# Tail of a hybrid layer issued by two parts of the tokens, and its low-rank products as two split passes on 128 rows

## The chip, the core and the metric

The kernel runs on one core of one Trainium2 chip. The metric is the device time of the whole program in microseconds (us). TensorE (PE) multiplies, with PEld as its weight loads; VectorE (DVE), ScalarE (ACT) and GpSimd (POOL) do the elementwise work; SyncE (SP) mostly issues DMA transfers.

## The reference

Two layers over 768 tokens (256 of context, then 512 latents); the second layer needs its output for the latents alone. D = 1024, D_FF = 4096.

```python
for l in range(DEPTH):                       # DEPTH = 2
    h = modulate(x, norm_mix_pre[l], shift0, scale0)          # rms_norm(x, g) * (1 + scale) + shift
    o = token_mixer(h, ...)     # w_in -> rwkv (decay, iclr: low-rank), conv, attention -> w_branch, gates, w_out
    x = x + mod2 * rms_norm(o, norm_mix_post[l])
    h = modulate(x, norm_mlp_pre[l], shift1, scale1)
    x = x + mod5 * rms_norm(square(relu(h @ w_ff1[l])) @ w_ff2[l], norm_mlp_post[l])
# low-rank, d = 0, 1:  w_raw = w0[d] + tanh(wd) @ w2[d];  a = sigmoid(a0[d] + ad @ a2[d])   (64 x 1024 each)
```

Context and latents have modulation vectors of their own. The output is the latents' x in float32.

## The kernel before

Activations lie transposed, channels on the partitions in KT = 8 tiles of 128, tokens along the free axis. A layer has T = 768 tokens (layer 0) or 512 (layer 1, the latents alone).

**Large products.** Every large product is done as three fp32r products of parts that are each rounded: weight-hi by activation-hi (`wh`, `hh`), weight-hi by activation-lo (`hl`), weight-lo (`wl`) by activation-hi. One job is one output tile of 128 channels: 8 k-tiles, 3 products each, over one or two pieces of the tokens (2 x 384 in layer 0, one of 512 in layer 1). `gemm` (L378, product L389) issues a whole job; `job` and `fill` (L392 to L414, product L412) keep jobs in a list, from which other parts of the program take a few k-steps at a time, so that products lie between other work.

**Weights.** A job takes two weight halves (`weight_half`, L369): an SP DMA of 256 KB into `raw` (L372), a ring of two buffers; ACT rounds it into `wh` (L328); DVE subtracts to get `wl` (L332). `wh` and `wl` have three buffers each. A slot of `raw` is free again after the DVE subtraction.

**The tail of a layer.** `merge_phase` (L1237) ends with the 8 jobs of `w_out` into `acc`. Then, in `mlp_phase` (L1335): load X (the residual stream) from DRAM, post-norm with gate and add to X, sums of squares of X, norm and modulation into `hh`, `hl` (`norm_h`, L334, its first step L343), 4 quarters q of the MLP (8 jobs of `w_ff1`, 8 of `w_ff2` each), post-norm and add again, and in layer 0 the norm for layer 1 and the store of X to DRAM (`xT_d`, L1392), in layer 1 the transposes and the store of the output (`store_x`). Row sums of squares go through PE by a vector of ones (L311; squares by ACT at L306 and L320). `rstd` (L281) takes them to ACT (L287), PE (L291), DVE (L279) and back by PE transposes (L298) as `mm`; the post-norm is a DVE scalar_tensor_tensor (L359) and an add (L361) on DVE or POOL. In `mlp_phase` all of this is for all tokens at once. The mod steps (L234: a `wmod` load of 1 MB and 4 products each) make the next layer's modulation, one after each job of `w_ff1`.

**The low-rank products.** For each of 8 head pairs and each layer `rw_open` (L1021) loads `lw` (two DMAs on SP, L1025), and `rw_lora` (L1028, product L1032) multiplies 64 rows of `lw` (one direction) by 64 rows of `low`, in float32.

**Spills.** 36 output tiles of `w_in` (queries, keys, values, gates) are made as jobs between the steps of the rwkv branch and written to a DRAM tensor `z` (`spill`, L1155).

The order is that of the Python program, on which a tile framework's scheduler then settles each engine's order.

Of the kernel before, what the change touches and what calls it, by code (L numbers as in the profile page):

```python
# [76 lines left out]
class Kern:  # L77
# [255 lines left out]

    def norm_h(s, sp, X, R, T, gs, sh, hh, hl):  # L334

        nc = s.nc
        o = TOK - T
        for k in range(KT):
            t = sp.tile([128, TOK], F32, tag="nt", name="nt", bufs=2)
            for b, t0, t1 in s.pieces(T, CTX):  # L340
                v = 1 if t0 < CTX else 0
                sl = slice(t0, t1)
                nc.vector.scalar_tensor_tensor(out=t[:, sl], in0=X[:, k, sl], scalar=gs[:, k, v:v + 1], in1=R[:, b, :t1 - t0], op0=ALU.mult, op1=ALU.mult)  # L343
                if k % 2:
                    nc.scalar.activation(out=t[:, sl], in_=t[:, sl], func=AF.Identity, bias=sh[:, k, v:v + 1])
                else:
                    nc.scalar.activation(out=hh[:, k, sl], in_=t[:, sl], func=AF.Identity, bias=sh[:, k, v:v + 1])  # L347
                    nc.vector.scalar_tensor_tensor(out=hl[:, k, sl], in0=t[:, sl], scalar=sh[:, k, v:v + 1], in1=hh[:, k, sl].bitcast(F32), op0=ALU.add, op1=ALU.subtract)
            if k % 2:
                s.split(hh[:, k, o:], hl[:, k, o:], t[:, o:], True)  # L350

    def post_norm(s, sp, A, X, R, T, gm, each):

        nc = s.nc
        o = TOK - T
        for k in range(KT):
# [35 lines left out]
    def job(s, src, mh, ml, T, done, pre=None):  # L392

        s.halves += [(src, h) for h in range(2)]
        s.jobs += [(k, mh, ml, T, done, pre) for k in range(KT)]

    def fill(s, n=1):
        nc = s.nc
        for _ in range(min(n, len(s.jobs))):
            k, mh, ml, T, done, pre = s.jobs.pop(0)  # L400
# [243 lines left out]
    def stage(s):  # L644
        return s.wp.tile([128, TOK], F32, tag="f0", name="f0", bufs=2)
# [25 lines left out]
    def rw_loras(s, l, P, T):  # L671
        nc = s.nc
        s.sgd = s.rp.tile([128, TOK], F32, name="sgd")
        s.low = s.rp.tile([128, 2, TOK], F32, name="low")
        s.shift_mix(l, P, C_WD, TOK, lambda: s.low[:, 0])
        s.shift_mix(l, P, C_AD, TOK, lambda: s.low[:, 1])
        s.shift_mix(l, P, C_GD, T, lambda: s.sgd)
        s.fill(24)
        nc.scalar.activation(out=s.low[:, 0], in_=s.low[:, 0], func=AF.Tanh)
# [341 lines left out]
    def rw_open(s, l, p):  # L1021

        lw = s.rt("lw", [128, 2, 128])
        for i, n in ((0, 'rw_w2'), (1, 'rw_a2')):
            s.nc.sync.dma_start(lw[:, i, :], s.i[n][l, :, :, 128 * p:128 * p + 128].rearrange("d r n -> (d r) n"))  # L1025
# [37 lines left out]
    def spill(s, l, r, T):  # L1063

        c0, t, f = s.spills[r]
        T = TOK if t else T
        s.in_job(l, c0, T, lambda ps: s.spill_done(r, T, f, ps))

    def spill_done(s, r, T, tanh, ps):
        nc = s.nc  # L1070
        ft = s.stage()
        if tanh:
            nc.scalar.activation(out=s.dv(ft, T), in_=s.pv(ps, T), func=AF.Tanh, scale=0.5)
        else:
            nc.scalar.activation(out=s.dv(ft, T), in_=s.pv(ps, T), func=AF.Copy)
        nc.scalar.dma_start(s.z[128 * r:128 * r + 128, TOK - T:], ft[:, TOK - T:])


    def run(s):
# [13 lines left out]
        s.z = s.dp.tile([128 * len(s.spills), TOK], F32, name="z")  # L1093
        s.kp = lambda d: d.rearrange("(k p) t -> p k t", p=128)
# [15 lines left out]
        for l in range(DEPTH):  # L1110
# [5 lines left out]
            s.h_open()  # L1116
            s.mlp_phase(l, PP, T, acc, actx)
# [9 lines left out]
    def rwkv_phase(s, l, P, T):  # L1127
# [3 lines left out]
        with ExitStack() as rc:  # L1131
# [105 lines left out]
    def merge_phase(s, l, PP, T, acc):  # L1237
# [4 lines left out]
        with ExitStack() as mc:  # L1242
# [67 lines left out]
            drive(ln, 3)  # L1310
            s.fill(len(s.jobs))
            branch(1, *operand(lambda k: cvx[k]))
            for j in range(KT):
                s.fill(8)
                if steps:
                    steps.pop(0)()
            for k in range(KT):
                nc.vector.tensor_scalar(out=acc[:, k, o:], in0=acc[:, k, o:], scalar1=0.5, scalar2=None, op0=ALU.mult)
            hs, ls = operand(lambda k: acc[:, k])
            s.ss = s.ps2()  # L1320

            def done(j, ps):
                nc.scalar.activation(out=s.dv(acc[:, j], T), in_=s.pv(ps, T), func=AF.Copy)
                s.ss_slow(lp, s.ss, acc[:, j], j, T)
            for j in range(KT):
# [121 lines left out]
```

## Time and profile before

| | |
|---|---|
| median of 3 runs | 4390.17 us (4380.69 to 4404.21) |
| the profiled execution | 4402.83 us, span 4401.0 us |
| PE busy | 4180.3 us, 95% of the span |
| DVE, ACT, POOL busy | 2707.6, 1819.4, 289.9 us |

The profile holds one execution. A span is what lies between its first and its last instruction; the time of the execution is 1.8 us longer. Busy time is summed by engine, and "the chain" is the work that ended last, followed back step by step.

### The profile page before, as it was taken

The page shows a single profiled execution, that of the slowest core. Times are in us where ns is not written, and L with a number is a line of the kernel's source. Part 1 is how long each engine was busy: PE and PEld are TensorE (multiplying, and loading weights), DVE is VectorE, ACT ScalarE, POOL GpSimd, SP SyncE. Part 2 cuts the span into 40 slices and gives each one's busy share as a digit, 9 for nine tenths or more (in the row PEclk, how much of TensorE's full clock was granted, in tenths as well). Part 3 has the DMA queues.
Part 4 walks back from the last instruction along what each step waited for, and adds up shares of the span by engine and source line. Part 5 has one row for each costly group of instructions (what it writes and reads, how often), then busy time and mean ns, then how long its engine had stood idle before and what let it go on. Part 6 is the DMA issues. An engine that isn't in the chain of part 4 may idle for free.

```text
span 4401.0 us, 76934 instructions
## 1 busy us (share of the span) xinstructions
PE 4180.3 (95%) x31232; PEld 3410.6 (77%) x31232; DVE 2707.6 (62%) x5214; ACT 1819.4 (41%) x3562; POOL 289.9 (7%) x349
## 2 busy tenths in 40 slices
PE   6999999999998989899999899999999989898998
PEld 4888888888886669689999677877777765575886
DVE  3778888878865564332233578888878755454344
ACT  3444444444434442332223345555444534433332
POOL 0000000000001022100000100000000001121001
PEclk9999999999999999899999889999999979998998
DMA  4212111111134235343322221121221232142332
GB/s 167 64 43 65 54 60 55 56 50 60 59 101 157 74 103 162 124 146 121 105 87 64 69 64 54 53 64 55 60 63 52 64 121 79 58 144 60 96 96 79
DMA packets 438346, 364.05 MB, mean 83 GB/s; under 512 B 19022, under 2 KB 386792, under 8 KB 431848
## 3 DMA queue, kind: packets, MB, share of 16 engines
q1 hardware_dynamic: 417256, 279.43, 21.1%
q10 hardware_dynamic: 20736, 79.70, 5.0%
q8 instruction: 247, 4.05, 0.4%
q14 instruction: 107, 0.88, 0.1%
HBM read 299.29 MB, written 53.48 MB: 80 GB/s over the span
## 4 chain that ended last, share of the span: by engine, by line
PE 81%; DVE 8%; ACT 4%; issue 2%; POOL 2%; DMA 2%; SPq 0%; ACTq 0%; POOLq 0%; DVEq 0%
PE mm L412 32%; PE mm L389 20%; PE g L807 4%; PE g L633 2%; PE g L931 2%; PE g L920 2%; PE sp L952 2%; PE g L1032 2%; PE sp L956 1%; PE S L612 1%; PE yp L970 1%; PE g L842 1%; PE yp L968 1%; PE g L816 1%; PE g L234 1%
## 5 line engine op out<-in xcount | busy, mean ns | idle before, releaser
L328 ACT ACTIVATE wh<-raw 128x512 fp32r<-128x512 f32 x700 | 441.9, 631 | 1283.4 <-PE mm L412 590.6
L332 DVE TENSOR_TENSOR wl<-raw,wh 128x512 fp32r<-128x512 f32 x700 | 501.6, 718 | 710.7 <-ACT wh L328 699.1
L412 PE MATMUL mm<-hh,wh 128*128 128x384 f32 (+1 forms) x2072 | 654.2, 373 | 10.2 <-ACT hh L347 4.0
L412 PE MATMUL mm<-hl,wh 128*128 128x384 f32 (+1 forms) x2072 | 640.5, 368 | 7.5 <-POOL hl L330 7.5
L412 PE MATMUL mm<-hh,wl 128*128 128x384 f32 (+1 forms) x2072 | 639.3, 368 | 0.0
L471 DVE SCALAR_TENSOR_TENSOR cv<-u,dw,cv 128x783 f32<-128x783 f32 (+1 forms) x480 | 425.7, 887 | 2.7
L412 PEld LDWEIGHTS mm<-hh,wh 128*128 128x128 f32 x2072 | 379.5, 192 | 54.9 <-issue 6.4
L412 PEld LDWEIGHTS mm<-hl,wh 128*128 128x128 f32 x2072 | 383.7, 192 | 47.7 <-POOL hl L330 10.8
L412 PEld LDWEIGHTS mm<-hh,wl 128*128 128x128 f32 x2072 | 385.7, 193 | 36.7 <-issue 7.2
L412 PE MATMUL mm<-oh,wh 128*128 128x384 f32 (+1 forms) x768 | 253.1, 384 | 9.6 <-DVE acc L1273 6.0
L412 PE MATMUL mm<-ol,wh 128*128 128x384 f32 (+1 forms) x768 | 240.3, 365 | 10.0 <-POOL ol L330 10.0
L389 PE MATMUL mm<-hh,wh 128*128 128x384 f32 (+1 forms) x768 | 239.1, 366 | 6.4 <-ACT hh L347 3.6
L389 PE MATMUL mm<-hl,wh 128*128 128x384 f32 (+1 forms) x768 | 238.0, 364 | 5.5 <-POOL hl L330 5.0
L412 PE MATMUL mm<-oh,wl 128*128 128x384 f32 (+1 forms) x768 | 239.3, 365 | 0.0
L389 PE MATMUL mm<-hh,wl 128*128 128x384 f32 (+1 forms) x768 | 235.7, 362 | 0.0
L389 PE MATMUL mm<-fh,wh 128*128 128x384 f32 (+1 forms) x768 | 229.9, 353 | 0.0
L389 PE MATMUL mm<-fh,wl 128*128 128x384 f32 (+1 forms) x768 | 229.8, 353 | 0.0
L389 PE MATMUL mm<-fl,wh 128*128 128x384 f32 (+1 forms) x768 | 229.5, 352 | 0.0
L807 PEld LDWEIGHTS g<-KR,BK 64*128 64x128 f32 x1536 | 156.6, 206 | 36.8 <-issue 32.4
L412 PEld LDWEIGHTS mm<-oh,wh 128*128 128x128 f32 x768 | 139.9, 190 | 51.3 <-ACT wh L328 13.6
L807 PE MATMUL g<-KR,BK 64*128 64x128 f32 (+1 forms) x1536 | 176.4, 307 | 1.8 <-DVE KR L800 1.6
L958 ACT ACTIVATE S<-sp,lam 128x64 f32<-128x64 f32 x352 | 92.1, 310 | 191.6 <-PE sp L956 182.0
(293 smaller groups left out, 7215.0 us busy)
## 6 DMA issues: line engine op xcount, KB each, us to landing
raw<-in_w_in_dram SPq DMA_DIRECT2D x316, 256.0 KB
raw<-in_w_ff_dram SPq DMA_DIRECT2D x256, 256.0 KB
wmod<-in_w_mod_dram ACTq DMA_DIRECT2D x48, 1024.0 KB
raw<-in_w_branch_dram SPq DMA_DIRECT2D x96, 256.0 KB
z<-f ACTq DMA_DIRECT2D x40, 384.0 KB
gt<-z SPq DMA_DIRECT2D x24, 384.0 KB
raw<-in_w_out_dram SPq DMA_DIRECT2D x32, 256.0 KB
z<-f ACTq DMA_DIRECT2D x32, 256.0 KB
```

The costliest lines, as they stand in the source:

```text
L328: s.last_hi = nc.scalar.activation(out=hi, in_=src, func=AF.Copy)
L332: nc.vector.tensor_tensor(out=lo, in0=src, in1=hi.bitcast(F32), op=ALU.subtract)
L389: nc.tensor.matmul(ps[:, b, :t1 - t0], lhsT=w[:, k % 4, :], rhs=a[:, t0:t1], start=k == 0 and f == 0, stop=k == KT - 1 and f == 2)
L412: s.last_mm = nc.tensor.matmul(s.jps[:, b, :t1 - t0], lhsT=w[:, k % 4, :], rhs=a[:, t0:t1], start=k == 0 and f == 0, stop=k == KT - 1 and ...
L471: s.tap_pin(nc.vector.scalar_tensor_tensor(out=hold['c'], in0=u[:, k:k + L], scalar=w(k), in1=hold['c'], op0=ALU.mult, op1=ALU.add))
L633: nc.tensor.matmul(op[:, :nq], lhsT=V[:, kk, kv * 128:kv * 128 + 128], rhs=PT[:, kk, :nq], start=kk == 0, stop=kk == nk // 128 - 1)
L807: nc.tensor.matmul(gp[h][:, q, 0:n, :], lhsT=BK[ROWS[h], 4 * g + q].rearrange("p a b -> p (a b)"), rhs=KR[ROWS[h], 0:n, 4 * g + q, :], sta ...
L920: nc.tensor.matmul(wu[ROWS[h], q - q0], lhsT=TT[ROWS[h], q, :], rhs=KM[ROWS[h], q].rearrange("p a b -> p (a b)"), start=True, stop=True)
L931: nc.tensor.matmul(ap[ROWS[h], q - q0, 0:n, :], lhsT=W[ROWS[h], q, :], rhs=GB[ROWS[h], h, q, 0:n, :], start=True, stop=True)
L952: nc.tensor.matmul(sp[ROWS[h], d], lhsT=GB[d][:, h, q[d], 0, :], rhs=UV[d][:, h * 12 + q[d], :], start=d == 0, stop=d == 1 and k == 0)
L958: nc.scalar.activation(out=Sn[:, d], in_=sp[:, d], func=AF.Copy, scale=Q['lam', d][:, q[d]:q[d] + 1])
L1032: s.nc.tensor.matmul(o, lhsT=Q['lw'][ROWS[d], i, :], rhs=s.low[ROWS[d], i, t0:t1], start=True, stop=True)
```

## The change

- `tail_phase` replaces `w_out` in `merge_phase` and the whole of `mlp_phase`. `w_out`, the first quarter of `w_ff1` and the last quarter of `w_ff2` are issued by two parts of the tokens: layer 0 by 256 and 512 tokens (the last `w_ff2` by 256 and 2 x 256), layer 1 by 256 and 256. Each part's jobs load and split their weights again. All other quarters stay whole, as jobs.
- A generator, `residual`, does post-norm, add, sums, and the next norm of one part, and is woven between the jobs of the other part (after each yield some k-steps of the listed jobs are issued). `weight_half` is now at L442 (DMA L445, ACT L344, DVE L348), the product at L486, `rstd_p` at L371 (PE L380, L386), the row sums at L428, the mod step at L250.
- 8 of layer 1's gate spills (rows 28 to 35) are issued for the first 256 latents during layer 0's last norm, and for the other 256 later, in layer 1.
- The low-rank weights go into one slot of the `raw` ring (four DMAs of 32 KB), and are split into hi and lo by ACT and DVE; `low` becomes four tiles that hold the 64 hi rows of one direction above or below its 64 lo rows (one half brought by a DMA from SBUF to SBUF), and a product is two fp32r passes over 128 rows. The buffer `f0` of `stage` goes from 2 to 1.
- The steps of the convolution's LayerNorm and the mod steps in `merge_phase` get other spacings, and all adds to X are on DVE.

```diff
     def job(s, src, mh, ml, T, done, pre=None):
-        s.jobs += [(k, mh, ml, T, done, pre) for k in range(KT)]
+        s.jobs += [(k, mh, ml, T if isinstance(T, list) else s.pieces(T), done, pre) for k in range(KT)]
...
+    def residual(s, sp, A, X, ss, pcs, gm, nxt=None):
+        R = s.rstd_p(sp, ss, pcs)
+        yield 2.0
+        s2 = s.g([128, 512]) if nxt else None
+        for k in range(KT):
+            for t0, t1, r in R:
+                v = 1 if t0 < CTX else 0
+                nc.vector.scalar_tensor_tensor(out=A[:, k, t0:t1], in0=A[:, k, t0:t1], scalar=gm[:, k, v:v + 1], in1=r, op0=ALU.mult, op1=ALU.mult)
+            for t0, t1 in s.spans(pcs):
+                nc.vector.tensor_tensor(out=X[:, k, t0:t1], in0=X[:, k, t0:t1], in1=A[:, k, t0:t1], op=ALU.add)
+            if nxt:
+                sq, n = s.squares(sp, X[:, k], pcs)
+                nc.tensor.matmul(s2[0:1, :n], lhsT=s.ones, rhs=sq, start=k == 0, stop=k == KT - 1)
+            yield 0.5
+        if nxt:
+            R = s.rstd_p(sp, s2, pcs)
+            yield 2.0
+            for k in range(KT):
+                s.norm_k(sp, X, R, k, nxt[0], nxt[1], s.hh, s.hl)
+                yield 0.5
...
     def rw_open(s, l, p):
-        lw = s.rt("lw", [128, 2, 128])
+        raw = s.wp.tile([128, 4, 128], F32, tag="raw", name="lraw", bufs=s.nraw)
...
+        lw = [s.rp.tile([128, 4, 128], F32R, tag=f"lw{f}", name="lw", bufs=1) for f in range(2)]
+        s.split(lw[0], lw[1], raw)
...
     def rw_lora(s, Q, i, ds, t0, t1):
-            s.nc.tensor.matmul(o, lhsT=Q['lw'][ROWS[d], i, :], rhs=s.low[ROWS[d], i, t0:t1], start=True, stop=True)
+            for f in range(2):
+                s.nc.tensor.matmul(o, lhsT=Q['lw'][f][:, 2 * i + d, :], rhs=s.low[i, d][:, t0:t1], start=f == 0, stop=f == 1)
...
+        if T == TOK:
+            parts, ends = ([(0, 0, CTX)], [(0, CTX, TOK)]), ([(0, CTX, 512)], [(0, 0, CTX), (1, 512, TOK)])
+        else:
+            parts = ends = ([(0, CTX, 512)], [(0, 512, TOK)])
...
+            out_jobs(parts[0], h[0])
+            flush()
+            out_jobs(parts[1], h[1])
+            s.weave(0.6, s.residual(sp, acc, X, h[0]['ss'], parts[0], P['gm'][0], nxt(P, 1)))
+            flush()
+            f0 = []
+            ff1_jobs(0, parts[0], f0)
+            s.weave(0.6, s.residual(sp, acc, X, h[1]['ss'], parts[1], P['gm'][0], nxt(P, 1)))
+            flush()
...
+            ff1_jobs(0, parts[1], f0, each)
+            ff2_jobs(0, full, f0)
+            flush()
...
+            ff2_jobs(3, ends[0], fs, h[0])
+            flush()
+            ff2_jobs(3, ends[1], fs, h[1])
+            s.weave(0.6, s.residual(sp, acc, X, h[0]['ss'], ends[0], P['gm'][1], n))
...
+            flush()
+            if not last:
+                for r in s.early:
+                    s.spill(l + 1, r, ends[0])
+            s.weave(0.6, s.residual(sp, acc, X, h[1]['ss'], ends[1], P['gm'][1], n))
```

On PE, layer 1, between `w_out` and the MLP: `mm` is a product's output, `S` the norm spread over the partitions, `g` a row sum (by L311 and L428) or a column of `rstd`. Before:

```order
L412 MATMUL mm<-oh,wl 128x512
L311 MATMUL S<-sq,ones 1x512
L291 MATMUL g<-ones,row 128x1 x4
L298 MATMUL mm<-cst,rs 128x128 x4
L311 MATMUL S<-sq,ones 1x512 x8
L291 MATMUL g<-ones,row 128x1 x4
L298 MATMUL mm<-cst,rs 128x128 x4
L389 MATMUL mm<-hh,wh 128x512
```

And after, the second part's norm beside the first part's `w_ff1`:

```order
L486 MATMUL mm<-hl,wh 128x256
L386 MATMUL S<-cst,rs 128x128 x2
L486 MATMUL mm<-hh,wl 128x256
L486 MATMUL mm<-hh,wh 128x256
L486 MATMUL mm<-hl,wh 128x256
L428 MATMUL g<-sq,ones 1x256 x8
L486 MATMUL mm<-hh,wl 128x256
L486 MATMUL mm<-hh,wh 128x256
L486 MATMUL mm<-hl,wh 128x256
L486 MATMUL mm<-hh,wl 128x256
L380 MATMUL g<-ones,row 128x1 x2
```

Products now stand among the norm's own; the 8 row sums stand together, three products after the transposes.

On PE, layer 0, the same place after the change (the second part, 512 tokens; `wmod` is a mod step's load, L192 and L193 bring layer 1's parameters):

```order
L486 MATMUL mm<-hh,wh 128x256
L486 MATMUL mm<-hl,wh 128x256
L486 MATMUL mm<-hh,wl 128x256
L428 MATMUL g<-sq,ones 1x512 x8
L380 MATMUL g<-ones,row 128x1 x4
L192 MATMUL g<-cst,ra 128x128
L193 MATMUL g<-cst,rb 128x77
L250 MATMUL g<-wmod,sc_18391 32x512 x8
L386 MATMUL S<-cst,rs 128x128 x4
L250 MATMUL g<-wmod,sc_18391 32x512 x16
L486 MATMUL mm<-hh,wh 128x256
```

Six of the 24 mod steps (4 products each) now stand here, two ahead of the transposes of the second norm and four behind them, ahead of the products that follow; before, each stood behind a job of `w_ff1`.

On SP, the end of layer 0, before (`xT_d<-X` is the store of X, 3 MB; `raw` are weight halves, L372 before and L445 after):

```order
L372 DMA raw<-in_w_ff_dram 128x4x128 x123
L372 DMA raw<-in_w_in_dram 128x4x128 x5
L1392 DMA xT_d<-X 128x8x768
L372 DMA raw<-in_w_in_dram 128x4x128
L1025 DMA lw<-in_rw_w_dram 128x128
```

And after:

```order
L445 DMA raw<-in_w_out_dram 128x4x128 x21
L445 DMA raw<-in_w_ff_dram 128x4x128 x160
L445 DMA raw<-in_w_in_dram 128x4x128 x8
L1529 DMA xT_d<-X 128x8x768
L445 DMA raw<-in_w_in_dram 128x4x128 x4
L1123 DMA g_26296<-in_rw_g_dram 128x128
```

Layer 0's MLP issues 160 halves in this row where it issued 128 in two, and the store stands behind 8 of the early spills' 16 halves.

## Rows read from the trace of the kernel before

**Rows 1.** The page: span, busy time by engine, the chain's shares, the clock by slices.

```profile
span 4401.0 us, 76934 instructions
...
PE 4180.3 (95%) x31232; PEld 3410.6 (77%) x31232; DVE 2707.6 (62%) x5214; ACT 1819.4 (41%) x3562; POOL 289.9 (7%) x349
...
PEclk9999999999999999899999889999999979998998
...
PE 81%; DVE 8%; ACT 4%; issue 2%; POOL 2%; DMA 2%; SPq 0%; ACTq 0%; POOLq 0%; DVEq 0%
```

**Rows 2.** The chain in order of time: start, duration, engine, line, count.

```profile
2241.56 191.97 PE mm L389 x1100
...
4016.80 347.69 PE mm L389 x1496
...
4368.40 3.65 PE mm L389 x15
```

**Rows 3.** Windows: us, busy PE, PEld, DVE, ACT, POOL, clock, DMA share, GB/s.

```profile
1828.40:1877.80 49.40, 31.48 (x117) 15.86 (x116) 33.04 (x79) 20.93 (x34) 10.87 (x6) 0.76 0.20 69
2444.50:2499.00 54.50, 36.90 (x128) 20.69 (x128) 35.77 (x71) 22.68 (x35) 13.10 (x8) 0.75 0.18 68
3977.80:4008.00 30.20, 17.73 (x46) 6.22 (x45) 15.13 (x41) 9.96 (x16) 6.60 (x4) 0.68 0.06 18
4371.50:4402.00 30.50, 12.87 (x49) 7.99 (x47) 13.11 (x29) 3.60 (x6) 6.60 (x4) 0.60 0.17 69
```

**Rows 4.** Timeline of layer 1's w_branch: weight halves on SP, ACT and DVE.

```profile
3862.98 1.85 SPq L372 DMA_DIRECT2D raw<-in_w_branch_dram  x2
3867.65 4.71 SPq L372 DMA_DIRECT2D raw<-in_w_branch_dram  x3
...
3867.79 0.63 ACT L328 ACTIVATE wh<-raw 128x512 fp32r<-128x512 f32 x1 [0.89 <-DMA raw<-in_w_branch_dram]
3870.61 0.63 ACT L328 ACTIVATE wh<-raw 128x512 fp32r<-128x512 f32 x1 [2.18 <-DMA raw<-in_w_branch_dram]
...
3871.27 0.69 DVE L332 TENSOR_TENSOR wl<-raw,wh 128x512 fp32r<-128x512 f32 x1 [0.19 <-ACT wh L328]
```

**Rows 5.** Timeline of the norm after layer 1's w_out.

```profile
3977.80 0.40 PE L412 MATMUL mm<-oh,wl 128*128 128x512 f32 x1
...
3980.95 0.59 ACT L287 ACTIVATE row<-S 1x512 f32<-1x512 f32 x1 [1.11 <-PE S L311]
...
3987.05 1.41 DVE L359 SCALAR_TENSOR_TENSOR acc<-acc,mc,mm 128x512 f32<-128x512 f32 x2 [1.21 <-PE mm L298]
```

**Rows 6.** Groups by form on DVE, the last norms: busy, mean ns | idle before.

```profile
L359 DVE SCALAR_TENSOR_TENSOR acc<-acc,mc,mm 128x512 f32<-128x512 f32 x8 | 5.6, 742 | 1.2 <-PE mm L298 1.2
L361 DVE TENSOR_TENSOR X<-X,acc 128x512 f32<-128x512 f32 x4 | 2.7, 684 | 0.0
...
L359 DVE SCALAR_TENSOR_TENSOR acc<-acc,mc,mm 128x256 f32<-128x256 f32 x8 | 3.8, 472 | 1.7 <-PE mm L298 1.7
```

**Rows 7.** Windows: one mod step's load, the store of X, two stretches of w_branch.

```profile
1702.60:1706.20 3.60, 3.60 (x23) 3.60 (x22) 1.02 (x2) 0.54 (x1) 0.00 (x0) 1.00 0.94 316
2470.00:2480.00 10.00, 5.44 (x27) 3.38 (x26) 5.05 (x18) 2.70 (x5) 0.00 (x0) 0.81 0.79 311
3750.00:3770.00 20.00, 18.40 (x73) 11.03 (x72) 9.41 (x20) 9.38 (x20) 0.00 (x0) 1.00 0.13 40
3810.00:3830.00 20.00, 13.27 (x50) 8.54 (x48) 9.91 (x14) 8.73 (x16) 13.44 (x11) 0.86 0.34 106
```

**Rows 8.** Timeline on PE: low-rank products beside others.

```profile
262.21 0.91 PE L1032 MATMUL g<-low,lw 64*128 64x384 f32 x2
263.05 0.33 PE L970 MATMUL yp<-UV,GB 128*64 128x64 f32 x2
433.03 0.92 PE L1032 MATMUL g<-low,lw 64*128 64x384 f32 x4
433.87 0.45 PE L412 MATMUL mm<-hl,wh 128*128 128x384 f32 x1
```

More of the change, by code (lines that the diff above doesn't have):

```diff
@@ new lines, in rstd_p @@
+    def rstd_p(s, sp, ss, pcs):
+        nc = s.nc
+        n = sum(t1 - t0 for b, t0, t1 in pcs)
+        row = sp.tile([128, TOK], F32, tag="sq", name="row", bufs=2)[0:1]
+        nc.scalar.activation(out=row[:, :n], in_=ss[0:1, :n], func=AF.Copy, scale=1.0 / D)
+        cps = s.g([128, 8])
+        m = n // 128
+        for t in range(m):
+            nc.tensor.matmul(cps[:, t:t + 1], lhsT=row[0:1, t * 128:(t + 1) * 128], rhs=s.ones[0:1, 0:1], start=True, stop=True)
+        rs = sp.tile([128, 8], F32, tag="rs", name="rs", bufs=2)
+        nc.vector.tensor_scalar(out=rs[:, :m], in0=cps[:, :m], scalar1=EPS, scalar2=None, op0=ALU.add)
+        s.rsqrt(rs[:, :m], s.rq[:, 0, :m], s.rq[:, 1, :m])
+        R = s.ps2()[:, 0]
+        for t in range(m):
+            nc.tensor.transpose(out=R[:, t * 128:t * 128 + 128], in_=rs[:, t:t + 1].to_broadcast([128, 128]), identity=s.ident)
+        out, o = [], 0
+        for b, t0, t1 in pcs:
+            out.append((t0, t1, R[:, o:o + t1 - t0]))
+            o += t1 - t0
+        return out
@@ new lines, in squares, with ss_tile @@
+    def squares(s, sp, x, pcs):
+        sq, o = sp.tile([128, TOK], F32, tag="sq", name="sq", bufs=2), 0
+        for t0, t1 in s.spans(pcs):
+            s.nc.scalar.activation(out=sq[:, o:o + t1 - t0], in_=x[:, t0:t1], func=AF.Square)
+            o += t1 - t0
+        return sq[:, :o], o
+    def ss_tile(s, sp, hold, x, k, pcs):
+        sq, n = s.squares(sp, x, pcs)
+        if k == 0:
+            hold['sa'] = sp.tile([128, 512], F32, tag="sa", name="sa", bufs=1)[:, :n]
+            s.nc.gpsimd.tensor_copy(hold['sa'], sq)
+        elif k < KT - 1:
+            s.nc.gpsimd.tensor_tensor(out=hold['sa'], in0=hold['sa'], in1=sq, op=ALU.add)
+        if k >= KT - 2:
+            if k == KT - 2:
+                hold['ss'] = s.g([128, 512])
+            s.nc.tensor.matmul(hold['ss'][0:1, :n], lhsT=s.ones, rhs=hold['sa'] if k == KT - 2 else sq, start=k == KT - 2, stop=k == KT - 1)
@@ L1309, in merge_phase @@
             branch(2, *operand(load(s.oat)))
-            drive(ln, 3)
-            s.fill(len(s.jobs))
+            for _ in range(4):
+                for _ in ln:
+                    s.fill(3)
+                    break
+            while s.jobs:
+                for _ in range(2):
+                    next(ln, None)
+                s.fill(8)
+                if steps:
+                    steps.pop(0)()
+            for _ in ln:
+                pass
             branch(1, *operand(lambda k: cvx[k]))
@@ L1314, in merge_phase, with tail_phase @@
                 s.fill(8)
[L1315 to L1325, printed above, removed]
[L1326 to L1330 removed]
+                for _ in range(2 if len(steps) > KT - j else 1):
+                    if steps:
+                        steps.pop(0)()
             if l == 0:
                 s.mod_post(P)
[L1333 to L1335 removed]
+    def tail_phase(s, l, PP, T, acc):
         nc, tc, i, P = s.nc, s.tc, s.i, PP[l]
@@ new lines, in ff2_jobs, with done @@
+            def ff2_jobs(q, pcs, fs, hold=None):
+                def done(j, ps):
+                    for t, p in s.views(ps, pcs, acc[:, j]):
+                        if q == 0:
+                            nc.scalar.activation(out=t, in_=p, func=AF.Copy)
+                        else:
+                            nc.vector.tensor_tensor(out=t, in0=p, in1=t, op=ALU.add)
+                    if hold is not None:
+                        s.ss_tile(sp, hold, acc[:, j], j, pcs)
+                for j in range(KT):
+                    s.job(i['w_ff2'][l, q * D:(q + 1) * D, 128 * j:128 * j + 128], lambda k: fs[k][0], lambda k: fs[k][1], pcs, lambda ps, j=j: done(j, ps))
```

211 lines of the change are left out of this document (116 added, 95 removed).

## Prediction

> **What bounds the kernel now.** I began with the page. Within the span of 4401.0 us PE is busy 95%, and the chain that ended last lies on PE for 81% [rows 1]. So first come the products, then the stretches in which PE is not fed; the clock digits are 9 almost everywhere, with a few 7s and 8s [rows 1]. The chain in order of time gives the price of a product: 191.97 us for 1100 in layer 0, 0.1745 each over 384 tokens, and 347.69 for 1496 in layer 1, 0.2324 over 512 [rows 2]. A job of 48 products in layer 0 is thus 8.38 us, one of 24 in layer 1 is 5.58.
>
> The windows show what the tail's norms cost [rows 3]. After layer 0's `w_out` stand 49.4 us in which PE does 117 instructions, none of them a large product; after its MLP 54.5. In layer 1 the last product of `w_out` starts at 3977.80 [rows 5]; the chain is back in the products at 4016.80 with 1496 of them, and 15 more stand at 4368.40 [rows 2], so 25 of the 1536 (64 jobs of 24) lie before: 39.0 - 25 x 0.2324 = 33. The last norm and the store take 30.5 [rows 3]. **These four stops are 167 us, all that weaving the norms could win.**
>
> The third thing read is the weight ring. Beside layer 1's `w_branch` SP issues halves at 3862.98 (two) and 3867.65 (three, over 4.71) [rows 4]. A slot comes back when its half has landed (the ACT split at 3870.61 was released by the DMA, after 2.18 idle), ACT has taken 0.63 and DVE 0.69 [rows 4]. Two halves thus need 4.67 us from 3862.98 to 3867.65; the shortest such round that I found is within the second row, whose third issue is 4.34 behind its first. One job needs two halves. Today that hides behind jobs of 5.58 and 8.38.
>
> **The change, part by part.**
>
> *Stages in two parts.* I price 256 tokens by the straight line through 384 and 512: 0.1745 - (0.2324 - 0.1745) = 0.117, between 0.116 and, if nothing were saved under 384 tokens, 0.1745. A job of 24 is then 2.8 us of PE (at most 4.2), but its two weight halves take a ring round of 4.34 to 4.67. A 256-token job is therefore paced by the ring; I take 4.5, and 5.0 as the upper bound, since DVE and ACT do the norm's work in between. A layer 0 stage was 8 x 8.38 = 67.0 us and becomes 8 x 4.5 + 8 x 5.58 = 80.6, so +13.6 for `w_out` and for the first `w_ff1`; the last `w_ff2` has 48 products of 0.117 = 5.6 in its second part, +13.8. In layer 1 a stage was 8 x 5.58 = 44.6 and becomes 16 x 4.5 = 72, +27.4, three times. Sum: 41 + 82 = **+123**. There are 72 such jobs, so 4.34 gives 11.5 less and 5.0 gives 36 more.
>
> *The stops that go.* **-167**, worked out above.
>
> *The stops that come.* From the last product to the first post-norm step is 3977.80 to 3987.05, 9.2 us [rows 5]; of these the stretch from the row at 3980.95 on is 6.1, so a second norm within a chain is some 7 with its sums. A post-norm and add is 0.742 + 0.684 over 512 tokens, and 0.472 plus some 0.4 over 256 [rows 6]; eight k are 11.4 and 7.0. The order on PE puts eight row sums together, three products behind the transposes: PE then stands still for the whole k loop although other products follow. So:
> - Layer 0, second part beside the first `w_ff1`: 9.2 + 11.4 + 1.5 for the last square and sum + 7 = 29 until the second set of transposes. Behind it stand four mod steps; there are two `wmod` buffers, and the loads are queued on ACT behind the norm's own activations: 8 x 2 x 0.742 for the norm [rows 6] and one load of 3.6 us [rows 7] make 15, until 44. Products done meanwhile: 53, and at the ring's pace (48 products in 9.0) they give back 9.9; the halves that the ring brings meanwhile return some 4. I take 30.
> - Layer 0, last norm: 9.2 + 8 x (2 x 0.472 + 0.684) + 1.2 = 23.4 until X is whole. The store of X stands on SP before the last 8 halves of the early spills; 3 MB took 10.0 us at 311 GB/s [rows 7], and the 8 halves then need 8 x 2.25 = 18. With one more round of about 5 for the next job: 57. The early products lie inside it.
> - Layer 1, second part: the k loop of 7.0 and 5 for the ring to turn again: 12. Its last norm: 9.2 + 7.0 + 5.3 for half of the store, which had been about 30.5 - 9.2 - 11.4 = 10: 21.5.
> - The four first parts lie beside the other part's jobs, with the same bunched sums; I put 5 and 5 in layer 0, 8 and 8 in layer 1. Loading X beside `w_out`'s halves takes 4, since 3 MB go through the same queue in pieces.
>
> Sum: 30 + 57 + 12 + 21.5 + 26 + 4 = **+150**. The new stops give back nearly all that the old ones cost.
>
> *Work that moves.* Eight early jobs leave 256 instead of 512 tokens in layer 1's rwkv stretch: 8 x (5.58 - 2.8) = -22; there the products stand among other work, so their ring round is covered. If that cover is gone, it is 8 x (5.58 - 4.5) = 9 only. Mod steps now inside stops save some 6: **-28** together.
>
> *Low-rank products.* A float32 product over 384 tokens leaves two records and holds PE from 262.21 to 263.05, 0.84; the two directions together, four records on two halves of the rows, hold it from 433.03 to 433.87, 0.84 too [rows 8]. A head pair has two such pairs and four single ones in a layer, 6 x 0.84 = 5.05 us. After the change these are 16 passes; at the large products' 0.1745 they take 2.8, and I take 3.4, since each of them changes its weights and stands alone. Sixteen pairs: **-26** (0 if the rwkv recurrence covers them, -36 at 2.8). The new splits, 0.63 + 0.69 [rows 4] sixteen times, lie in the idle half of ACT and third of DVE [rows 1]; uncovered they would cost 21. Each layer starts with four copies of the low halves on SP, with weight halves queued behind them: +5 each, **+10** (0 to 20). The single `f0` buffer I put at 0: an ACT copy and its DMA are short beside a job of 5.58; uncovered, each of the 72 spills would wait for its store, some 2 us as a half's landing takes [rows 4], 144 in all, and it is the cost that I know least.
>
> Sum: 123 - 167 + 150 - 28 - 26 + 10 = +62. Against the profiled 4402.8 us that is 4465; the median is 12.7 below that execution, so 4452, and I say **4450**.
>
> **The rivals.**
> - *The forecast*, the ring paces the 256-token jobs and the stops return in other places: 4450, between 4410 and 4505 with the ring's bounds and a third of the stops. Chance 0.58.
> - *The new stops are hidden.* During a stop the ring fills three halves ahead, which later jobs then needn't wait for; if a third of the 150 is absorbed (-52), the time is about 4400. For it: the norm's own DVE work of 20 us leaves time for `wh` to be ready. Against it: three `wh` buffers hold only one and a half jobs. Chance 0.25.
> - *The ring doesn't pace* (faster). If halves return sooner once PE no longer waits, a job takes 2.8 and not 4.5: 72 x 1.7 = 122 less, 4330 to 4340. It decides from a round of about 3.6 us per job: there 72 x 0.9 = 65 equals the forecast's loss. Against it: every round in the rows is 4.3 or more. Chance 0.09.
> - *The lower clock.* PE was granted 1.00 in a stretch where it was busy 18.40 of 20 us, 0.86 where it was busy 13.27 [rows 7], and 0.76 in the norm after `w_out` [rows 3]. A ring-paced stage is busy 2.8 of 4.5. If it fell to the lower of the two levels (1.2 GHz of 2.4) a product would take 0.234 and a job 5.6, above the ring's 4.5: the 72 jobs and the 8 early ones x 1.1 = +88, about 4540. At 0.86 it is 0.136 and 3.3, and nothing changes. The Trainium skill, "TensorE: Matmul & The Clock Gate", section "HAM oscillation — how this bites in real kernels", says that bursts of products shorter than the waits for their data can run at the lower clock each time; these stages would be such bursts, and the 0.86 speaks for a part of it only. Chance 0.08.
>
> **How the numbers follow.** About 0.5%, 22 us, is what a measurement here can tell from no change: faster is below 4368, slower above 4412. Faster takes the third rival and a part of the second, 0.17; same takes most of the second and the forecast's low edge, 0.22; slower the rest, 0.61. The range goes from 4362, which holds the second rival with the low-rank bound, to 4520, short of the lower clock.
>
> **What would show it.** In the stages of 256 tokens: 24 products per 4.3 to 5 us, PE at some 60%, and SP issuing the next half when DVE's split ends. In layer 0's MLP a stop of about 30 after the row sums, with PE waiting on `wmod`; at its end a wait on a weight half behind the store of X. PE's total busy time should change little. In the low-rank products, two fp32r passes in less than one float32 product. The forecast is wrong if 256-token jobs come at under 3.6 us each, if PE's idle time in the stops beside the other part is near 0, or if the start of layer 1 or the rwkv stretch grows by more than 20 (a cost that I have not found).

## The result and the profile after

The changed kernel took 4495.01 us (median of 4 runs, 4485.79 to 4498.09) against 4390.36 (4380.69 to 4404.21): slower, ratio 1.0237 (95% interval 1.0211 to 1.0263). The forecast was 4450, range 4362 to 4520. The profiled execution of the changed kernel, 4485.79 us, is 9 below its median where that of before was 12.5 above its own, so the two traces differ by 83 us and the medians by 104.6.

The windows divide both spans by the same events: the last product of `w_in` in each layer (taken as the end of its rwkv stretch), the first load of `w_out`, the last product of `w_ff2`. Columns are as in [rows 3]. Before (layer 0's rwkv, its `w_branch`, its tail; the same for layer 1, whose fourth window begins with layer 0's last norm):

```profile
69.00:1354.00 1285.00, 1264.44 (x12209) 1085.52 (x12210) 994.89 (x1972) 585.73 (x1229) 37.24 (x104) 0.98 0.20 61
1354.00:1731.00 377.00, 350.38 (x1684) 268.68 (x1683) 208.46 (x356) 160.69 (x301) 62.34 (x34) 0.98 0.38 124
1731.00:2444.00 713.00, 691.03 (x3921) 635.17 (x3920) 229.51 (x331) 195.41 (x286) 53.13 (x35) 0.98 0.34 109
2444.00:3612.00 1168.00, 1126.99 (x10391) 884.97 (x10390) 896.08 (x1907) 566.54 (x1204) 47.46 (x107) 0.93 0.20 61
3612.00:3919.00 307.00, 266.08 (x1005) 173.13 (x1004) 167.19 (x293) 128.58 (x244) 44.68 (x32) 0.94 0.32 101
3919.00:4401.00 482.00, 447.07 (x1861) 347.88 (x1859) 198.73 (x317) 166.46 (x275) 44.36 (x31) 0.94 0.30 88
```

After:

```profile
68.00:1329.00 1261.00, 1241.55 (x12212) 1086.58 (x12211) 998.66 (x1983) 593.82 (x1245) 35.14 (x108) 0.99 0.21 64
1329.00:1713.00 384.00, 360.01 (x1749) 268.85 (x1748) 204.70 (x358) 160.56 (x301) 61.19 (x35) 0.98 0.43 142
1713.00:2456.00 743.00, 707.39 (x4073) 626.88 (x4072) 288.60 (x500) 241.07 (x415) 49.47 (x50) 0.98 0.35 110
2456.00:3629.00 1173.00, 1116.00 (x10550) 904.12 (x10549) 904.80 (x1933) 577.22 (x1247) 37.92 (x107) 0.92 0.22 66
3629.00:3942.00 313.00, 263.03 (x1011) 170.70 (x1011) 169.79 (x308) 129.45 (x247) 45.29 (x31) 0.95 0.32 100
3942.00:4484.00 542.00, 476.24 (x2461) 390.20 (x2459) 252.50 (x481) 205.81 (x387) 32.08 (x40) 0.95 0.34 102
```

The two tails are longer by 30 and 60 us, although the norms in them now have products beside them. Layer 0's `w_branch` is 7 longer: 8 of the mod steps that stood beside `w_out` stand there now. Layer 0's rwkv stretch is 24 shorter; layer 1's, which should have won by the low-rank products and by the spills made early, is 5 longer. In layer 1 of the changed kernel the last product of `w_in` ends 8 us before the rwkv branch stores its output; before, both ended together. By that store the stretch grows from 1167.8 to 1181.0 us, by 13, and the `w_branch` behind it is 2 shorter.

**The weight ring.** Layer 1's first `w_ff1` quarter, a stretch with no norm in it, on SP, ACT and PE (the rows that answer to [rows 4]):

```profile
4082.13 10.78 SPq L445 DMA_DIRECT2D raw<-in_w_ff_dram  x6
```
```profile
4084.95 0.63 ACT L344 ACTIVATE wh<-raw 128x512 fp32r<-128x512 f32 x1 [1.54 <-DMA raw<-in_w_ff_dram]
4085.66 0.38 ACT L1458 ACTIVATE f<-mm 128x256 f32<-128x256 f32 x1
...
4089.09 0.63 ACT L344 ACTIVATE wh<-raw 128x512 fp32r<-128x512 f32 x1 [1.47 <-DMA raw<-in_w_ff_dram]
```
```profile
4080.20 0.28 PE L486 MATMUL mm<-hh,wh 128*128 128x256 f32 x1
4080.32 0.28 PE L486 MATMUL mm<-hl,wh 128*128 128x256 f32 x1
4080.43 0.28 PE L486 MATMUL mm<-hh,wl 128*128 128x256 f32 x1
4081.43 0.39 PE L486 MATMUL mm<-hh,wh 128*128 128x256 f32 x1 [0.72 <-ACT wh L344]
...
4082.16 0.38 PE L486 MATMUL mm<-hh,wl 128*128 128x256 f32 x1 [0.23 <-DVE wl L348]
```

Products start 0.12 apart, so a job would be 2.8 us; PE then waits for ACT's split, ACT for the load. From one job's split that a load released to the next job's is 4.14 us (4084.95 to 4089.09).

**The longest stop.** Layer 0, the second part's norm beside the first `w_ff1`, on PE:

```profile
1839.11 0.28 PE L486 MATMUL mm<-hh,wl 128*128 128x256 f32 x1
1841.55 7.05 PE L428 MATMUL g<-sq,ones 128*1 128x512 f32 x12 [2.17 <-ACT sq L397]
...
1859.20 1.65 PE L250 MATMUL g<-wmod,sc 128*32 128x512 f32 x8 [2.91 <-DMA wmod<-in_w_mod_dram]
...
1869.52 1.94 PE L250 MATMUL g<-wmod,sc 128*32 128x512 f32 x8 [1.83 <-DMA wmod<-in_w_mod_dram]
1871.39 0.58 PE L486 MATMUL mm<-hh,wh 128*128 128x256 f32 x1
```

No large product for 32.3 us: the eight row sums follow the norm's k loop, then six mod steps, four of them waiting for their loads.

**Low-rank products** (on PE, answering to [rows 8]): four passes, two products, hold PE from 143.67 to 144.38, 0.71 us.

```profile
143.67 0.88 PE L1118 MATMUL g<-low,lw 128*128 128x384 f32 x4
144.38 0.52 PE L486 MATMUL mm<-hh,wh 128*128 128x384 f32 x2
```

### The profile page after: what moved, and what is told of

Same layout as the page of the kernel before. It is cut to its first block, busy times and chain, and to the rows that moved or that the text cites. A ratio compares the mean times of both kernels' runs of the same rounds, so it can differ in the third digit from the quotient of the medians.

```text
span 4484.0 us, 80243 instructions
## 1 busy us (share of the span) xinstructions
PE 4198.6 (94%) x32216; PEld 3463.6 (77%) x32216; DVE 2832.4 (63%) x5602; ACT 1924.4 (43%) x3865; POOL 261.8 (6%) x377
## 5 line engine op out<-in xcount | busy, mean ns | idle before, releaser
L344 ACT ACTIVATE wh<-raw 128x512 fp32r<-128x512 f32 x812 | 511.0, 630 | 1268.7 <-PE mm L486 962.0
L348 DVE TENSOR_TENSOR wl<-raw,wh 128x512 fp32r<-128x512 f32 x812 | 577.0, 712 | 706.0 <-ACT wh L344 690.6
L486 PE MATMUL mm<-hh,wh 128*128 128x384 f32 (+2 forms) x2968 | 924.2, 362 | 41.7 <-ACT wh L344 25.0
L486 PE MATMUL mm<-hh,wl 128*128 128x384 f32 (+2 forms) x2968 | 911.8, 359 | 13.7 <-DVE wl L348 13.5
L486 PE MATMUL mm<-hl,wh 128*128 128x384 f32 (+2 forms) x2968 | 908.0, 357 | 1.8 <-POOL hl L346 1.8
L486 PEld LDWEIGHTS mm<-hh,wh 128*128 128x128 f32 x2968 | 550.5, 193 | 113.0 <-ACT wh L344 39.3
L486 PEld LDWEIGHTS mm<-hh,wl 128*128 128x128 f32 x2968 | 554.8, 193 | 65.0 <-DVE wl L348 22.5
L486 PEld LDWEIGHTS mm<-hl,wh 128*128 128x128 f32 x2968 | 555.9, 193 | 42.4 <-POOL hl L346 3.0
L486 PE MATMUL mm<-fh,wh 128*128 128x256 f32 (+2 forms) x1152 | 340.5, 332 | 25.4 <-ACT wh L344 20.8
L486 PE MATMUL mm<-fh,wl 128*128 128x256 f32 (+2 forms) x1152 | 341.7, 333 | 10.8 <-DVE wl L348 10.4
L486 PE MATMUL mm<-fl,wh 128*128 128x256 f32 (+2 forms) x1152 | 337.8, 329 | 3.9 <-POOL fl L346 3.0
L486 PEld LDWEIGHTS mm<-fh,wh 128*128 128x128 f32 x1152 | 214.5, 193 | 47.9 <-ACT wh L344 29.0
L486 PEld LDWEIGHTS mm<-fh,wl 128*128 128x128 f32 x1152 | 214.9, 193 | 32.1 <-DVE wl L348 19.1
L486 PEld LDWEIGHTS mm<-fl,wh 128*128 128x128 f32 x1152 | 215.2, 193 | 19.5 <-issue 4.4
L486 PE MATMUL mm<-oh,wh 128*128 128x384 f32 (+1 forms) x576 | 193.6, 391 | 9.3 <-DVE acc L1364 6.0
L486 PE MATMUL mm<-ol,wh 128*128 128x384 f32 (+1 forms) x576 | 180.4, 365 | 6.9 <-POOL ol L346 6.9
L486 PE MATMUL mm<-oh,wl 128*128 128x384 f32 (+1 forms) x576 | 180.0, 365 | 0.0
```

Of the source, the lines that this page charges most:

```text
L344: s.last_hi = nc.scalar.activation(out=hi, in_=src, func=AF.Copy)
L348: nc.vector.tensor_tensor(out=lo, in0=src, in1=hi.bitcast(F32), op=ALU.subtract)
```

## The experiments

Each is the changed kernel with the edit shown, unless said otherwise. Ratios are to the kernel before. The last column is the lowest and the highest mean granted clock of the row's executions; those of the kernel before lie between 0.959 and 0.969.

| | median us | ratio (95%) | granted clock |
|---|---|---|---|
| the change | 4495.0 | 1.0237 (1.0211 to 1.0263) | 0.958 to 0.962 |
| four raw slots in the tail | 4416.7 | 1.0063 (1.0041 to 1.0086) | 0.959 to 0.964 |
| rate 2.4 beside norms | 4461.6 | 1.0165 (1.0136 to 1.0194) | 0.962 to 0.967 |
| late mod steps | 4493.2 | 1.0232 (1.0209 to 1.0255) | 0.960 to 0.962 |
| layer 1's tail whole | 4424.9 | 1.0077 (1.0050 to 1.0103) | 0.960 to 0.963 |
| low-rank part alone | 4373.2 | 0.9949 (0.9934 to 0.9964) | 0.963 to 0.964 |
| four slots and rate 2.4 | 4407.8 | 1.0035 (1.0017 to 1.0052) | 0.961 to 0.967 |
| store of X from ACT | 4482.1 | 1.0204 (1.0186 to 1.0222) | 0.962 to 0.964 |
| no early spills | 4464.5 | 1.0162 (1.0141 to 1.0183) | 0.961 to 0.967 |
| four mends | 4379.4 | 0.9975 (0.9959 to 0.9992) | 0.964 to 0.970 |
| four mends, late mod steps | 4384.2 | 0.9984 (0.9968 to 0.9999) | 0.963 to 0.970 |
| tail part alone | 4496.7 | 1.0242 (1.0216 to 1.0268) | 0.964 to 0.967 |
| tail part alone, no early spills | 4486.5 | 1.0208 (1.0187 to 1.0229) | 0.962 to 0.966 |

**The granted clock beside the medians.** Executions of one kernel differ with their mean granted clock: beside the tail alone, the kernel before took 4402.98 us at 0.960 and 4378.59 at 0.967. Inside a profile the same is seen where two kernels run the same program, as from layer 1's first whole product to the store of the rwkv output in the changed kernel and in the one with the store of X from ACT (10318 instructions on PE in both):

```profile
2513.80:3637.70 1123.90, 1078.14 (x10318) 875.43 (x10318) 873.11 (x1853) 551.66 (x1187) 31.05 (x91) 0.92 0.21 63
2518.50:3632.50 1114.00, 1064.61 (x10318) 863.54 (x10318) 873.00 (x1853) 552.34 (x1187) 30.98 (x91) 0.94 0.22 63
```

That is 9.9 us at 0.92 against 0.94. Rows with few executions ran at different clocks, so a difference of 10 to 30 us between their medians need not be the edit's. Below, executions at the same clock stand beside such differences. How much of an execution's clock is the kernel's own doing, by its stops, is not shown.

**Four raw slots in the tail.**

```diff
-        raw = s.wp.tile([128, 4, 128], F32, tag="raw", name="raw", bufs=s.nraw)
+        s.hn += 1
+        raw = s.tp.tile([128, 4, 128], F32, tag="rawt", name="raw", bufs=2) if s.tp and s.hn % 2 else s.wp.tile([128, 4, 128], F32, tag="raw", name="raw", bufs=s.nraw)
```

> In the tail every second weight half goes into two buffers of their own, so that the raw ring has four slots there instead of two; nothing else changes. Theory (the ring of two paces the 256-token jobs: 4.1 us per job in the profile of the changed kernel against 2.8 us of products): the 72 jobs fall to about 2.9 us each, 72 x 1.2 = 86 us less, of which the stops take a part back; 4405 to 4430 us, and PE busy over 90% in those stages. Rival (the 256-token jobs are paced by the splits on ACT and DVE, or by the products themselves): within 15 us of 4495.

78 us less; at clock 0.962, 69 (4416.40 against 4485.79). In a window of layer 1's 256-token jobs PE is now busy throughout at clock 1.00:

```profile
4050.00:4090.00 40.00, 40.00 (x323) 39.28 (x322) 28.45 (x56) 25.03 (x54) 0.00 (x0) 1.00 0.64 183
```

Its 323 products in 40.00 us are 2.97 per 24, where the changed kernel had 209 in 34 us, 3.9 per 24:

```profile
4066.00:4100.00 34.00, 30.63 (x209) 26.70 (x208) 17.17 (x33) 16.01 (x34) 0.00 (x0) 0.97 0.40 116
```

The ring paced those jobs; neither the splits' own work nor the products did. The new slots lie in the tail's memory pool, and the first half of `w_out` came late for it, which cost part of the gain:

```profile
1753.42 0.58 PE L487 MATMUL mm<-fh,wh 128*128 128x256 f32 x1 [16.92 <-ACT wh L344]
```

**Rate 2.4 beside norms** (in all four places).

```diff
-            s.weave(0.6, s.residual(sp, acc, X, h[0]['ss'], parts[0], P['gm'][0], nxt(P, 1)))
+            s.weave(2.4, s.residual(sp, acc, X, h[0]['ss'], parts[0], P['gm'][0], nxt(P, 1)))
```

> The rate at which k-steps of the other part are issued beside a norm goes from 0.6 to 2.4 per estimated us, in all four places of the tail. Theory (PE stops because only some 7 k-steps of products stand between the norm's own PE instructions, and the rest of the other part's jobs stands behind them): the stops of 7.5 and 11 us in layer 1 and the first 10 us of the stop of 32 us in layer 0 mostly close; 15 to 35 us less, 4460 to 4480. Rival (the stops are set by the weight ring, or by the mod steps' loads, whatever the order): within 10 us of 4495.

33 us less by the medians, but 11 at clock 0.962 (4474.48 against 4485.79). In layer 1's tail the longest stretch without a large product is now 7.2 us, where the changed kernel had stops of 7.5 and 11.0 in the same norm and of 5.7 and 5.5 in others; layer 0's stop of 32.3 became 9.5 and 16.9. By windows cut as above layer 1's tail is 525 us instead of 543, layer 0's 748 instead of 744. So the order on PE made the stops of layer 1; in layer 0 something else ends the later part.

**Late mod steps.**

```diff
-                nc.gpsimd.memset(st['sc'], 0.0)
+                if late is not None:
+                    nc.gpsimd.tensor_scalar(out=st['sc'], in0=late.rearrange('p (a b) -> p a b', b=32), scalar1=0.0, scalar2=None, op0=ALU.mult)
+                else:
+                    nc.gpsimd.memset(st['sc'], 0.0)
...
+                steps = [f for g in range(3) for f in s.mod_steps(l + 1, N, sp, g, 2, s.hl[:, 7, 512:768].bitcast(F32))]
```

> The first mod step of the next layer is made to depend on the end of the second part's norm, so that the six mod steps that stood around that norm's transposes come later, one after each job. Theory (in the stop of 32 us the last 12 to 15 us are four mod steps waiting for 1 MB loads that are queued on ACT behind the norm's activations, with products ready behind them): 8 to 14 us less, about 4484. Rival (the weight ring is empty there anyway, or the same wait moves to the next job): within 4 us of 4495.

The theory fell: 1.8 us less, and at clock 0.962 no less at all (4488.69 and 4490.89 against 4485.79). Without the mod steps the next product stood still as long, for another reason (on PE):

```profile
1870.90 0.58 PE L489 MATMUL mm<-hh,wh 128*128 128x256 f32 x1 [13.20 <-ACT f L1461]
```

It needed an output buffer that ACT had yet to empty, and in the changed kernel that eviction stands on ACT among the norm's activations, one row ahead of the norm's last split:

```profile
1868.62 0.72 ACT L365 ACTIVATE nt<-nt,mod 128x512 f32<-128x512 f32 x1 [1.17 <-DVE nt L363]
1869.24 0.36 ACT L1458 ACTIVATE f<-mm 128x256 f32<-128x256 f32 x1
1869.51 0.62 ACT L344 ACTIVATE hh<-nt 128x512 fp32r<-128x512 f32 x1
```

Two waits ended within 2 us of each other; the profile names the one that came last.

**Layer 1's tail whole.**

```diff
-            parts = ends = ([(0, CTX, 512)], [(0, 512, TOK)])
+            parts = ends = (full, [])
```

> Layer 1's tail is issued whole again (one part of 512 tokens, norms with nothing beside them), layer 0 stays in two parts. Theory: three stages of 16 x 4.1 us go back to 44.6 us, 63 less; the stops beside and between parts (some 40) go, and the whole norm stops of 33 and 30.5 come back; 45 to 65 us less in all, about 4440. Rival (layer 1's two parts win what the weaving promises and the loss is in layer 0 or in the rwkv stretch): 4500 or more.

70 us less, and 67 at clock 0.962 (4419.29 against 4485.79), a little over the bound. By the windows layer 1's tail is 479 us, against 482 before and 543 in the changed kernel: its two parts lose all that the tail had grown.

**The low-rank part alone**, in the kernel before (its diff is that of `rw_loras`, `rw_open`, `rw_lora` and `stage`).

> The kernel before with the low-rank part of the change alone (two fp32r passes on 128 rows, their weights through the raw ring and split, the low halves by SP copies, one buffer of f0), and its own tail. Theory (a head pair's products fall from 5.05 to 3.4 us, which the profile of the changed kernel bears out with 55 us for all 16 pairs against 81; the splits, copies and the single f0 buffer cost little): 15 to 28 us less than before, 4362 to 4376. Rival (the raw ring's slots and the single f0 buffer take the gain back, as layer 1's rwkv stretch of the changed kernel, no shorter than before, would suggest): within 8 us of 4390.

20 us less; at clock 0.964 some 13 to 17 (4369.71 and 4372.34 against 4385.52 to 4386.54). By windows cut at the same events, layer 0's rwkv stretch went from 1285 to 1267 and layer 1's from 1168 to 1162, and everything else stayed within 2.

```profile
69.00:1336.00 1267.00, 1246.26 (x12212) 1090.84 (x12212) 1002.41 (x1985) 594.87 (x1242) 34.34 (x104) 0.98 0.21 63
...
2424.00:3586.00 1162.00, 1110.24 (x10388) 882.09 (x10389) 904.48 (x1919) 573.65 (x1216) 46.88 (x107) 0.94 0.21 63
```

**Four slots and rate 2.4.**

```diff
             out_jobs(parts[0], h[0])
+            s.fill(16)
+            s.tp = sp
             flush()
```

> The changed kernel with the four raw slots in the tail (from the third job of w_out on, so that the first halves needn't wait for memory of the stage before) and the rate 2.4 beside norms. Theory (both causes hold and add up, and the late start of 16 and 9 us that the four slots alone showed at w_out is avoided): 4495 - 78 - 33 - 20 = 4360 to 4385. Rival (a faster ring empties the other part's jobs sooner, so that the stops grow and the gains overlap): 4395 to 4415.

The rival held: 9 us below the four slots alone by the medians, 3 to 4 at clock 0.962 (4412.12 and 4413.20 against 4416.40). The late first half of `w_out` is gone, and the gains overlap, perhaps because a faster ring leaves fewer products beside a norm. In layer 1 a stop of 8.2 us ends again with an eviction:

```profile
4018.01 0.40 PE L386 MATMUL S<-cst,rs 128*128 128x128 f32 x2 [1.97 <-DVE rs L295]
4023.96 0.58 PE L487 MATMUL mm<-hh,wh 128*128 128x256 f32 x1 [5.54 <-ACT f L1460]
```

**The store of X from ACT.**

```diff
-                nc.sync.dma_start(s.kp(s.xT_d), X)
+                nc.scalar.dma_start(s.kp(s.xT_d), X)
```

> The store of X at the end of layer 0 is issued from ACT instead of SP; nothing else changes. Theory (the stop of 9.5 us near the end of layer 0 is a weight half queued behind the 3 MB store on SP): 6 to 12 us less, about 4486. Rival (the halves still share the DMA engines with the store, or wait for the norm): within 4 us of 4495.

13 us less by the medians, which is not shown to be the store's: at 0.962 to 0.964 this kernel took 4481.40 to 4490.67, the changed kernel 4485.79 at 0.962. In the changed kernel an early product had waited for a weight half there:

```profile
2482.31 0.62 PE L386 MATMUL S<-cst,rs 128*128 128x128 f32 x4 [0.45 <-DVE rs L295]
2491.04 0.58 PE L486 MATMUL mm<-hh,wh 128*128 128x256 f32 x1 [8.11 <-ACT wh L344]
```

With the store on ACT the same wait is 5.56 us:

```profile
2493.47 0.58 PE L486 MATMUL mm<-hh,wh 128*128 128x256 f32 x1 [5.56 <-ACT wh L344]
```

Layer 1's first whole product comes 55.5 us behind layer 0's last one instead of 57.1. Behind it the two profiles differ by the 9.9 us of the two windows above, which are the same program at another clock.

**No early spills.**

```diff
-        s.early = list(range(28, 36))
+        s.early = []
```

> No early spills: the 8 gate tiles of layer 1 are made whole in layer 1, and nothing is woven beside layer 0's last norm. Theory (the early jobs put 22 us of products into a stop, and save 15 us in layer 1, where 192 products over 256 tokens take 40 us in place of 55, but each takes two halves a second time and they wait behind the store): the last norm's stop falls from 57 to some 40, layer 1 grows by 15, together within 8 us of 4495. Rival (the early jobs hide the norm as meant): 10 to 25 us more, 4505 to 4520.

Neither: 30 us less by the medians (4476.78 at clock 0.961, where the changed kernel took 4485.79 at 0.962). From the last `w_ff2` product to the next large product are 28.6 us (2471.3 to 2499.9), and layer 1's rwkv stretch with that norm, 1156 us, is shorter than with the early spills (1173), although it makes all 8 tiles whole.

```profile
2470.93 0.40 PE L486 MATMUL mm<-fl,wh 128*128 128x256 f32 x2
...
2499.93 1.65 PE L486 MATMUL mm<-hh,wh 128*128 128x384 f32 x4 [1.11 <-ACT hh L368]
```

In the changed kernel layer 1's first whole product stands at 2513.83, 57.1 us behind the end of layer 0's last one:

```profile
2513.83 0.62 PE L486 MATMUL mm<-hh,wh 128*128 128x384 f32 x2 [1.96 <-ACT wh L344]
```

So the early products make the stop 28.5 us longer. What they save behind it, with the same end as in the two windows above, is read at the same clock: without them 1127.80 us at 0.94, with them 1114.00 at 0.94.

```profile
2499.90:3627.70 1127.80, 1093.01 (x10316) 878.49 (x10316) 878.91 (x1871) 560.76 (x1205) 38.72 (x107) 0.94 0.21 62
```

They save 14 and cost 28.5.

**Four mends together, and five** (four slots, rate 2.4, no early spills, the store from ACT; then also the late mod steps).

> Four mends together: four raw slots in the tail, the rate 2.4, no early spills, the store of X on ACT. Theory (the two parts lose by the ring, the order beside the norms and the early jobs; with these mended the tail is worth a little, and the low-rank part gives its 20): 4407.8 - 30 for the early jobs = 4370 to 4385, the store adding nothing once no early halves stand behind it. Rival (the early jobs cost 30 only because of the ring of two, so that with four slots their removal gives little): 4395 to 4410.

> The four mends and the late mod steps as well. Theory (with the ring and the rate mended, four mod steps' loads are what ends last in the remaining stop of 15.6 us in layer 0, as the profile with two mends shows, while with the old order a product's eviction behind the norm's activations ended it at the same time): 4 to 10 us less than the four mends. Rival (the eviction of the next job's output still waits behind the norm's activations on ACT): within 3 us of it.

The four hold by the theory, 4379.4; but at clock 0.964 they took 4391.08, and the kernel before 4385.52 to 4386.54, so that a gain over it is not shown apart from the clock. The tails are 722 and 485 us, against 713 and 482 before and 743 and 542 after the change; the norm of layer 0's end lies in the next window. The fifth mend gives nothing: the rival's eviction again, or two waits that end together.

**The tail part alone, with and without the early spills** (low-rank products as before).

> The changed kernel with the low-rank part as before (float32 products on 64 rows, their own loads, two buffers of f0). Theory (the two parts of the change are independent, and the tail carries the whole loss): 4495 + 20 = 4508 to 4522. Rival (the tail's early spills and the raw ring suffer from the low-rank weights' slot and the single f0 buffer in layer 1, so that the two cost more together than apart): 4480 to 4500.

> The tail alone (float32 low-rank products and two f0 buffers, as before) without the early spills. It tells where the low-rank part's 20 us went in the changed kernel: alone they were there, inside the changed kernel only 2. Theory (they are lost to the early spills, which meet the low-rank weights and copies in the raw ring at the start of layer 1): without early spills the low-rank part gives its 20 again, so this kernel is 15 to 25 us above the 4464 of the same tail with the new low-rank products, 4478 to 4490. Rival (they are lost elsewhere, or the 20 is the spread of the runs): 4458 to 4472.

By the medians the tail alone is as slow as the whole change (4496.7 and 4495.0, in the rival's range), as if the low-rank part, worth 20 us alone, were worth 2 inside; without early spills it is worth 22 (4486.5 to 4464.5). But the tail alone ran at 0.964 to 0.967 and the changed kernel at 0.958 to 0.962. In the profiles layer 0's rwkv stretch, which lies ahead of all early spills, is 1278 us in the tail alone and 1260 in the changed kernel, both at 0.99: the same 18 as between 1285 and 1267. At 0.964 the low-rank part is worth 17 without early spills (4485.74 to 4468.50), and the early spills cost the tail alone 18 (4503.64 to 4485.74). So the gain is there in layer 0, and no run shows that the two parts take anything from each other.

## Why the forecast held, point by point

The direction and the main mechanism were right: the ring of two slots paces the 256-token jobs, and four slots give 78 of the 104.6 us back. At clock 0.962 that is 69 of some 93 (4485.79 against 4388.03 to 4398.19 before).

- **The ring's round** was taken at 4.5 us and measured 4.14 in the clear stretch, below even the low bound of 4.34; over 72 jobs that would be 26 less than +123. Whole stages came out as forecast all the same: layer 1's three, from the first product to the last and with their stops, take 80.8, 87.1 and 76.5 us where whole ones were priced at 44.6, together +110.6, and the forecast has 82 for the jobs and 28 for the stops. The price of 0.117 for a product over 256 tokens was right where it stands alone. PE's busy share was to be some 60% there; the window has 30.63 of 34 us, of which 209 products at 0.117 would fill 24.5.
- **The stops that go** (-167) were misread. The windows of 49.4 and 54.5 us were taken to hold no large product, but the first ones stand at 1863.76 and 2478.91 in the trace of before:

```profile
1863.76 1.01 PE L389 MATMUL mm<-hh,wh 128*128 128x384 f32 x2 [1.99 <-ACT hh L347]
2478.91 1.01 PE L412 MATMUL mm<-hh,wh 128*128 128x384 f32 x2 [1.99 <-ACT hh L347]
```

  The windows hold 30 and 53 such products, worth 5.2 and 9.2 us at 0.1745, so the term was some 14 too large. Without a large product were 35.7 and 34.6 us there, and 28.9 after layer 1's `w_out`.
- **The stops that come** (+150): layer 0's second part was forecast at 30 and is 32.3, for a reason that was half wrong (the mod steps' loads, which another wait covers). From layer 0's last product to layer 1's first whole one are 57.1, as forecast. Layer 1's second part was 12 and is 18.5; its last norm was 21.5 and is 20.3 (4463.7 to 4484.0).
- **The early spills** are the term that came out the wrong way. They were counted as -22 in layer 1, with their stop of 57 set against the misread 54.5. Their other parts, 192 products over 256 tokens in layer 1, take 31.6 us from start to start and wait 6.6 for their weight halves; over 512 tokens, at 0.28 each as the others there, they would be 53.8. So some 15 are saved, and the stop, 28.6 without them, is 57.1 with them: they cost where I booked a gain.
- **The low-rank products** went from 5.05 us a head pair, as priced, to 3.4, as forecast (55 us for the 16 pairs from start to start), and the net of -16 is -20 alone, some 15 at the same clock. The single `f0` buffer, the cost that I knew least, is inside that and did no harm that shows.
- **The rivals.** "Stops hidden" fell with the stops measured above, "the ring doesn't pace" with the four slots. The lower clock fell too: in the ring-paced stretch the granted clock is 0.97, in layer 0's stop of 32.3 us it is 0.76. The Trainium skill, "TensorE: Matmul & The Clock Gate", section "HAM oscillation — how this bites in real kernels", has bursts that are shorter than the waits between them run at the lower level each time. The trace doesn't show it here, where the waits were the shorter part: PE was busy 30.63 of 34 us, between waits of 0.2 to 0.7 us.

The forecast's sum was +62; the traces show +83 and the medians +104.6. Stage by stage its terms make -8 in layer 0's rwkv stretch, +28 in layer 0's tail, -28 from there to the store of layer 1's rwkv output, and +70 in layer 1's tail; the traces have -24, +30, +13 and +60, and 5 more in the two `w_branch` stretches. So the tails were forecast within 10. Layer 1's rwkv stretch is 41 off, some 20 of it by the misread window at layer 0's end, and layer 0's, 16 better than forecast, and layer 1's tail, 10 better, covered a part of that: that the total came as near as it did is luck to that extent. Of the 16, 8 are not the low-rank part's, since the tail alone, with the old products, has 1278 us there against 1285.

**Where the gain of weaving went.** With four mends the tail is about level with the old one: 9 and 3 us longer by the windows, with the stop at layer 0's end some 7 shorter. Less was to be hidden than the 167 us of the forecast; a stop of 16 us remains in layer 0's tail, one of 28 at its end and one of 20 at the end of the program, where nothing lies beside it, and each of the 72 jobs loads and splits two halves of its own. The version that beats both kernels by most is the low-rank part alone, 4373.2.

## What to carry to other kernels

Halving the tokens of a job halves its products but not its weight loads: divide the job's new time by the round of the buffers that feed it before splitting a stage. An order "beside" other work is worth only as many products as really stand between the waiting instructions on that engine; count them in the order, at their new size. Before a stop is put down to one wait, take it away: a second one may end at the same moment. Before a window is called a stop, look in it for the first product of what follows. Before two medians are compared, put the granted clocks of their executions beside them.

## What I hadn't expected

The Trainium skill, "Trainium Kernel Development and Optimization", section "Best Practices", asks for two buffers so that loads lie beside work. Here two were too few: a job took 4.14 us with two slots and 2.97 with four. And work made earlier in a stop, which looked free, made the stop 28.5 us longer and saved 14 behind it.
